# An encoder layer on one core: the fourth DRAM sum of w_o's blocks, and where the steps of the sums stand

## The chip, the cores and the metric

The kernel runs on one core of a Trainium2 chip. The metric is the device time of one execution in microseconds, the median of several runs. An engine is named as in the profile: PE (TensorE), PEld (its weight loads), DVE (VectorE), ACT (ScalarE), POOL (GpSimd), SP (SyncE, which here only issues transfers).

## The reference

One layer over 512 tokens of width 2048, all in float32:

```
h = rms_norm(x, pre_mix_g);  z = h @ w_in            # 2048 x 4096: q, k, v, u
a = chunked_attention(q, k, v, rel_bias)             # 8 heads of 128
p = multiscale_pool(u, pool_w, pool_scale)           # 4 groups of 256
m = concatenate([a, p]) @ w_o                        # 2048 x 2048
x = x + rms_norm(m, post_mix_g)
h = rms_norm(x, pre_ffn_g)
up = causal_dwconv(h @ w_up, conv_w, conv_b)         # 2048 x 11264, 3 taps
y = (gelu(up[:, :5632]) * up[:, 5632:]) @ w_down     # 5632 x 2048
x = x + rms_norm(y, post_ffn_g)
```

## The kernel before

Every float32 matrix is split into a rounded part (hi, written by ACT) and the rest (lo, written by DVE), and each product is three matmuls (`mm3`, L153 to L155). The split (L135, L136) of a weight tile needs the loaded tile (`raw4`, a ring of five) and a pair of buffers for hi and lo (`w4`, a ring of eight, so four pairs). `Weights` loads four tiles ahead: `get` of a tile first issues the load and the split of the tile four further on. A tile is 512 KB.

The stages are, in order of time: q, k, v and u projections with attention and pooling between them (the first 410 us); the product with w_o (410 to 575 us); the post-norm, the transposition back, and the first w_up products; then the w_up and w_down products, which fill the rest.

The product with w_o is made by a scheme of Strassen's kind with seven half-size products instead of eight, numbered in the order `WO = 1, 7, 2, 5, 6, 3, 4`. `wo_product(i, cc, left)` does half a product (column half `cc`, 0 or 1): four weight tiles `wo{i}_{cc}_0` to `_3`, 12 matmuls of 512 columns for each. The profile leaves numbers out, so all of them are called `wo_0` to `wo_3` there. The right factors are blocks of w_o or sums of them. Those of products 7, 5 and 6 are summed in DRAM (`wo_sum`, tiles `wt...`, in the profile `wt`). Product 4's right factor is sum 6 plus one more block. It isn't made in DRAM: `load_w` loads the block of w_o with SP, and POOL adds sum 6 to the loaded tile with an accumulating transfer (L148), before the split.

The sums in DRAM are made by a generator, `sums_in_dram`, one step at each `next(sums_step)`. A step is a copy from DRAM to DRAM, issued by SP (L251), or an accumulating transfer from DRAM onto DRAM, issued by POOL (L254), each of 1 MB. After w_o's 24 steps come 16 steps for w_down's first sums (`first_sum`, tiles `t...`, in the profile `t`), which are read near the end. The 24 steps stand among the heads of the attention, five of w_down's in the pooling stage, and the rest in the first w_up products, where `up` takes one step at each tile.

PE's instructions run in the order of the code. The other engines and queues are ordered by a scheduler, and each runs its own list in order: what stands behind a waiting instruction waits too. SP and POOL issue their transfers in such lists. `copy` is held behind the newest weight load; an add is placed where the scheduler expects its copy to be there, which may be earlier or later than its place in the code.

After product 4, for each half of the tokens (two tiles of 128): `finish` adds the product's banks to `y` (DVE, L582), squares it (ACT, L586) and scales it (DVE, L591); `norm` makes the factor, with a power on POOL (L643); `x2` updates x (DVE, L656); `turn_back` transposes x on PE (L670) and splits it into gT (L138, L139). For the first half this follows product 3, and its transposes stand between product 4's tiles in the second column half. For the second half it follows product 4, while PE does the first w_up tiles (w00) for the first half (`gate_part`). Then come the w10 tiles for all tokens.

Of the kernel before, what the change touches and what calls it, by code (L numbers as in the profile page):

```python
# [9 lines left out]
F32 = mybir.dt.float32  # L10
F32R = mybir.dt.float32r
AF = mybir.ActivationFunctionType
ALU = mybir.AluOpType
AX = mybir.AxisListType

P = 128
# [59 lines left out]
def encoder_layer(ctx: ExitStack, tc: tile.TileContext, x, xT, vecs, rel, post_mix, post_ffn,  # L76
# [7 lines left out]
    nc = tc.nc  # L84
# [8 lines left out]
    dram = ctx.enter_context(tc.tile_pool(name="dram", bufs=1, space=bass.MemoryType.DRAM))  # L93
# [7 lines left out]
    def bank(name):  # L101
        return psum.tile([P, 512], F32, tag="ps", name=name)

    def acc8(name, which, dt=F32):
        return acc.tile([P, 2048], dt, tag="acc" + which, bufs=2, name=name)

    def raw4(name):
        return big.tile([P, 1024], F32, tag="raw", bufs=5, name=name)

    def w4(name):  # L110
        return big.tile([P, 1024], F32R, tag="w4", bufs=8, name=name)
# [21 lines left out]
    def split(hi, lo, src, scale=None):  # L133
        if scale is None:
            rounded = nc.scalar.activation(hi, src, AF.Copy)  # L135
            nc.vector.tensor_sub(lo, src, f32(hi))  # L136
        else:
            rounded = nc.scalar.activation(hi, src, AF.Copy, scale=scale)  # L138
            nc.vector.scalar_tensor_tensor(lo, src, scale, f32(hi), op0=ALU.mult, op1=ALU.subtract)  # L139
        split.last = rounded.ins  # L140
        return rounded.ins

    def load_w(name, src, a, b, plus=None):
        n = a * b
        raw, hi, lo = raw4(name + "r"), w4(name + "h"), w4(name + "l")
        load_w.last = nc.sync.dma_start(raw[:, :n].rearrange("p (a b) -> p a b", a=a), src).ins
        if plus is not None:
            nc.gpsimd.dma_start(raw[:, :n].rearrange("p (a b) -> p a b", a=a), plus, accum_op=ALU.add)  # L148
        split(hi[:, :n], lo[:, :n], raw[:, :n])
        return tuple(v[:, :n].rearrange("p (a b) -> p a b", a=a) for v in (hi, lo))  # L150

    def mm3(ps, l, r, first, last):
        nc.tensor.matmul(ps, l[0], r[0], start=first, stop=False)  # L153
        nc.tensor.matmul(ps, l[0], r[1], start=False, stop=False)  # L154
        nc.tensor.matmul(ps, l[1], r[0], start=False, stop=last)  # L155
# [9 lines left out]
    def part(w, *idx):  # L165
        return tuple(v[(slice(None),) + idx] for v in w)
# [24 lines left out]
    def qk_specs(h):  # L191
        return halves(f"q{h}", w_in, head_cols("q", h), 8, P), halves(f"k{h}", w_in, head_cols("k", h), 8, P)
# [8 lines left out]


    WO = 1, 7, 2, 5, 6, 3, 4
    wo_sum = {i: [dram.tile([P, 8, 512], F32, name=f"wt{i}{cc}") for cc in range(2)] for i in (7, 5, 6)}

    def wo_block(cc, j, l):
        cs = slice(l * D // 2 + cc * 512, l * D // 2 + (cc + 1) * 512)
        return w_o[j * 1024:(j + 1) * 1024, cs].rearrange("(k p) n -> p k n", p=P)

    def wo_specs(i, cc):  # L210
        whole = wo_sum[i][cc] if i in wo_sum else wo_block(cc, *{1: (0, 0), 2: (1, 0), 3: (1, 1), 4: (1, 0)}[i])
        parts = [slice(2 * k, 2 * k + 2) for k in range(4)]
        return [(f"wo{i}_{cc}_{k}", whole[:, sl, :], 2, 512, *([wo_sum[6][cc][:, sl, :]] if i == 4 else []))
                for k, sl in enumerate(parts)]

    specs = v_specs(0)
    for h in range(1, HEADS):
        q, k = qk_specs(h)
# [24 lines left out]
    def first_block(cc, j, l):  # L243
        cs = slice(l * D // 2 + cc * S, l * D // 2 + (cc + 1) * S)
        return w_down[:2 * P * CU, cs].rearrange("(u j p) n -> p u j n", j=2, p=P)[:, :, j, :]

    def sums_in_dram():

        def copy(dest, source):
            with tc.issue_after(load_w.last):  # L250
                nc.sync.dma_start(dest, source)  # L251

        def add(dest, source):
            nc.gpsimd.dma_start(dest, source, accum_op=ALU.add)  # L254

        def wo_step(step, i, at):
            for cc in range(2):
                source = wo_block(cc, *at) if type(at) is tuple else wo_sum[at][cc]
                for k in range(2):
                    sl = slice(4 * k, 4 * k + 4)  # L260
                    step(wo_sum[i][cc][:, sl, :], source[:, sl, :])
                    yield

        for step, i, at in ((copy, 7, (1, 1)), (add, 7, (0, 1)), (copy, 5, (0, 0)), (add, 5, (0, 1)),
                            (copy, 6, 5), (add, 6, (1, 1))):
            yield from wo_step(step, i, at)
        for step, i, at in ((copy, 5, (0, 0)), (add, 5, (0, 1)), (copy, 7, (1, 1)), (copy, 6, 5),
                            (add, 7, (0, 1)), (add, 6, (1, 1)), (copy, 4, 6), (add, 4, (1, 0))):
            for cc in range(2):
                step(first_sum[i][cc], first_block(cc, *at) if type(at) is tuple else first_sum[at][cc])  # L270
                yield

    sums_step = sums_in_dram()


# [10 lines left out]
    for kb in range(KD):  # L286
        i, o = divmod(kb, 8)
        nc.sync.dma_start(xt[kb // 4][:, kb % 4, :], xT[kb * P:(kb + 1) * P, :])
        for what in "qk":
            if kb in chunks:  # L290
                raw, hi, lo = first[f"{what}0_{i}"]
                sl = slice(o * P, (o + chunks[kb]) * P)
# [4 lines left out]
        for what in "qk":  # L297
            _, hi, lo = first[f"{what}0_{i}"]
            sl = slice(o * P, (o + 1) * P)
# [7 lines left out]
    def mix(kb):  # L307
        return mixT[kb // 4][:, kb % 4, :]

    with tc.tile_pool(name="p1", bufs=2, reuse_waits="tile") as p1:  # L310
# [39 lines left out]
        def project(name, between=None):  # L350
            ps = bank(name)
            for i in range(2):
                if i and between:
                    between()
                w = weights.get(f"{name}_{i}")
                for j in range(8):
                    kb = 8 * i + j
                    mm3(ps, part(w, j), blk(hT, kb), kb == 0, kb == KD - 1)
            return ps
# [51 lines left out]
        def turn(h):  # L411
            probs = [state.pop(("p", h, t)) for t in range(NT)]
            pts = [bank(f"pt{h}_{k}") for k in range(3)]
            pts = [pts[0], pts[1][:, P:], pts[2][:, 2 * P:], pts[1][:, :P]]
            for k in (0, 1, 3, 2):
                for t in range(k, NT):
                    nc.tensor.transpose(pts[k][:, (t - k) * P:(t - k + 1) * P],
                                        probs[t][:, k * P:(k + 1) * P], ident)
            for k in range(NT):
                n, at = S - k * P, PT_AT[k] + k * P - PT_Q[k]  # L420
                split(pth[:, at:at + n], ptl[:, at:at + n], pts[k])

        def values(h):
            ps = bank(f"a{h}")
            d = slice((h % 4) * DH, (h % 4 + 1) * DH)
            for k in range(NT):
                sl = slice(PT_AT[k], PT_AT[k] + S - PT_Q[k])
                mm3(ps[:, PT_Q[k]:], part(state["v"], k, d), (pth[:, sl], ptl[:, sl]), k == 0, k == NT - 1)
            nc.scalar.activation(mix(h), ps, AF.Copy)

        def pool_proj(g, j):
            pool_keep(g, j, project(f"u{2 * g + j}"))
# [68 lines left out]
        turn(6)  # L501
        scores(7)
        pool_proj(0, 1)
        values(6)
        next(sums_step)
        pool_proj(1, 0)
        turn(7)
        pool_proj(1, 1)
        values(7)
        mixT += [acc8(f"mixT{i}", "B").rearrange("p (a b) -> p a b", a=4) for i in (2, 3)]  # L510
        pool_mix(0, keep_mix)
# [22 lines left out]

        def wo_product(i, cc, left, between=None):
            ps = [bank(f"m{i}{cc}{t}") for t in range(2)]
            for q in range(4):
                w = weights.get(f"wo{i}_{cc}_{q}")
                for j in range(2):
                    kb = 2 * q + j  # L540
                    for t in range(2):
                        mm3(ps[t], tuple(v[:, kb, t * P:(t + 1) * P] for v in left), part(w, j), kb == 0, kb == 7)
                if between:
                    between(q)
            return ps
# [13 lines left out]
    with tc.tile_pool(name="p2", bufs=1, reuse_waits="tile") as p2:  # L559
# [116 lines left out]
        whole = slice(0, D // 2)  # L676
# [165 lines left out]
    with tc.tile_pool(name="p3", bufs=2, reuse_waits="tile") as p3:  # L842
# [13 lines left out]
        def gate(u, z):  # L856
            a = p3.tile([P, 2, S], F32, tag="ca", name="ca")
            for j in range(2):
                taps(z[:, j, :], 2 * u + j, a[:, j, :])
            nc.scalar.activation(flat(a), flat(a), AF.Gelu_apprx_tanh)  # L860
            return a
# [13 lines left out]
        def normed(ps):  # L875
            z = new_z()
            for j in range(2):
                nc.vector.tensor_mul(z[:, j, :], ps[j], R)
            return z
# [207 lines left out]
        a = gate(1, normed(z))  # L1087
# [3 lines left out]
        a = gate(2, normed(z))  # L1091
# [272 lines left out]
```

## Time and profile before

| | |
|---|---|
| runs | 1932.14 us median of 3 (1931.54 to 1932.59) |
| profiled execution | 1932.79 us, its span from first to last instruction 1931.0 us |
| granted TensorE clock | 0.996 |
| PE busy | 1899.8 us of the span |
| DVE, ACT, POOL busy | 1432.8, 915.5, 285.3 us |
| DMA | 386.90 MB, mean 200 GB/s |

Busy time is what the engine's instructions took. A row of a timeline has the start and the duration in us, the engine, the line of the code, the operation, what is written and read, how many instructions the row holds, and in brackets how long the engine was idle before it and what ended that. A row of the windows has the window, its length, the busy time and the number of instructions of PE, PEld, DVE, ACT and POOL, the granted clock, the DMA share (the mean busy share of the core's 16 DMA engines) and GB/s. DMA rows name what is written and read, and the time from issue to landing.

### The profile page before, as it was taken

What the parts mean: (1) busy time and instruction counts of PE and PEld (TensorE: products, weight loads), DVE (VectorE), ACT (ScalarE), POOL (GpSimd) and SP (SyncE); (2) the same over time, 40 slices, a digit from 0 to 9 for tenths busy, and PEclk for the clock granted to TensorE, in tenths of its full rate; (3) what the DMA queues carried; (4) which work ended last, traced back from release to release, by engine and by line L of the source; (5) the groups of instructions that cost most, each with busy time, mean ns of one, the idle gap of its engine ahead of it and who ended that gap; (6) DMA issues with size and microseconds to landing.
All of it is one profiled execution on the core that took longest, in us unless ns stands there. A gap on an engine that the chain in (4) does not pass through costs nothing.

```text
span 1931.0 us, 28650 instructions
## 1 busy us (share of the span) xinstructions
PE 1899.8 (98%) x11566; PEld 1707.9 (88%) x11566; DVE 1432.8 (74%) x1618; ACT 915.5 (47%) x1126; POOL 285.3 (15%) x369
## 2 busy tenths in 40 slices
PE   9999999999979999999999999999999899999998
PEld 7888888888868889999999999999999688888886
DVE  5455345587668756887878878788788799998877
ACT  6333233356445434544544445444454655455543
POOL 5110010000010101111111111111110112222221
PEclk9999999999999999999999999999999999999999
DMA  7598395447695957667676676766766999999997
GB/s 244 162 259 217 120 264 142 133 148 250 188 305 184 287 144 162 155 170 188 150 188 157 168 188 150 186 161 166 188 162 196 324 265 250 255 210 240 227 222 238
DMA packets 182789, 386.90 MB, mean 200 GB/s; under 512 B 10944, under 2 KB 62528, under 8 KB 178624
## 3 DMA queue, kind: packets, MB, share of 16 engines
q1 hardware_dynamic: 132704, 249.79, 38.0%
q0 software_dynamic: 49952, 135.28, 37.1%
q8 instruction: 90, 1.47, 0.3%
q14 instruction: 43, 0.35, 0.1%
HBM read 328.40 MB, written 98.57 MB: 221 GB/s over the span
## 4 chain that ended last, share of the span: by engine, by line
PE 92%; DMA 3%; issue 2%; DVE 1%; ACT 1%; SPq 0%; POOL 0%; POOLq 0%; DVEq 0%; ACTq 0%
PE q L154 14%; PE q L153 14%; PE q L155 14%; PE p L155 6%; PE p L153 6%; PE p L154 6%; PE up L154 2%; PE up L155 2%; PE up L153 2%; PE m L153 2%; PE m L154 2%; PE m L155 2%; PE u L153 2%; PE v L153 2%; PE u L154 2%
## 5 line engine op out<-in xcount | busy, mean ns | idle before, releaser
L154 PE MATMUL q<-gTl,wfh 128*128 128x256 f32 x1216 | 344.1, 283 | 0.0
L155 PE MATMUL q<-gTh,wfl 128*128 128x256 f32 x1216 | 344.1, 283 | 0.0
L153 PE MATMUL q<-gTh,wfh 128*128 128x256 f32 x1216 | 344.1, 283 | 0.0
L153 PEld LDWEIGHTS q<-gTh,wfh 128*128 128x128 f32 x1216 | 233.5, 192 | 0.0
L154 PEld LDWEIGHTS q<-gTl,wfh 128*128 128x128 f32 x1216 | 233.5, 192 | 0.0
L155 PEld LDWEIGHTS q<-gTh,wfl 128*128 128x128 f32 x1216 | 233.5, 192 | 0.0
L153 PE MATMUL p<-bh,ah 128*128 128x512 f32 x560 | 219.3, 392 | 4.5 <-ACT ah L135 4.5
L154 PE MATMUL p<-bl,ah 128*128 128x512 f32 x560 | 219.1, 391 | 2.3 <-DVE bl L136 2.3
L155 PE MATMUL p<-bh,al 128*128 128x512 f32 x560 | 219.5, 392 | 1.7 <-DVE al L136 1.7
L135 ACT ACTIVATE wfh<-wx 128x1024 fp32r<-128x1024 f32 x152 | 159.9, 1056 | 119.1 <-PE q L154 91.4
L136 DVE TENSOR_TENSOR wfl<-wx,wfh 128x1024 fp32r<-128x1024 f32 x152 | 183.9, 1220 | 33.5 <-ACT wfh L135 33.4
L135 ACT ACTIVATE wfh<-wy 128x1024 fp32r<-128x1024 f32 x76 | 80.6, 1061 | 119.3 <-PE q L154 105.8
L135 ACT ACTIVATE bh<-b 128x2048 fp32r<-128x2048 f32 x56 | 106.9, 1917 | 61.3 <-DVE b L785 40.6
L136 DVE TENSOR_TENSOR bl<-b,bh 128x2048 fp32r<-128x2048 f32 x56 | 127.7, 2287 | 10.5 <-PE p L154 8.5
L153 PEld LDWEIGHTS p<-bh,ah 128*128 128x128 f32 x560 | 105.8, 189 | 27.1 <-ACT ah L135 5.3
L155 PEld LDWEIGHTS p<-bh,al 128*128 128x128 f32 x560 | 105.9, 189 | 24.8 <-DVE al L136 2.9
L997 POOL DMA_DIRECT2D wx<-in_w_up x76 | 67.5, 888 | 408.3 <-DVE wfl L136 381.5
L154 PEld LDWEIGHTS p<-bl,ah 128*128 128x128 f32 x560 | 105.8, 189 | 24.8 <-DVE bl L136 2.6
L136 DVE TENSOR_TENSOR wfl<-wy,wfh 128x1024 fp32r<-128x1024 f32 x76 | 92.9, 1223 | 32.2 <-ACT wfh L135 30.9
L837 POOL DMA_DIRECT2D sum<-part x60 | 72.7, 1231 | 251.4 <-DVE part L828 109.3
L136 DVE TENSOR_TENSOR wfl<-wz,wfh 128x1024 fp32r<-128x1024 f32 x38 | 46.6, 1225 | 59.7 <-ACT wfh L135 59.7
L153 PE MATMUL q<-h4h,wfh 128*128 128x256 f32 x304 | 86.0, 283 | 0.0
(590 smaller groups left out, 4953.7 us busy)
## 6 DMA issues: line engine op xcount, KB each, us to landing
wx<-in_w_up POOLq DMA_DIRECT2D x76, 512.0 KB, 7.0
sum<-part POOLq DMA_DIRECT2D x70, 512.0 KB, 8.2
b<-in_w_down SPq DMA_DIRECT2D x32, 1024.0 KB, 8.9
wx<-in_w_up SPq DMA_DIRECT2D x40, 512.0 KB, 6.1
wy<-in_w_up SPq DMA_DIRECT2D x38, 512.0 KB, 5.5
wz<-in_w_up SPq DMA_DIRECT2D x38, 512.0 KB, 7.0
wy<-in_w_up POOLq DMA_DIRECT2D x38, 512.0 KB, 7.4
wt<-in_w_o POOLq DMA_DIRECT2D x12, 1024.0 KB, 12.2
```

Of the source, the lines that this page charges most:

```text
L135: rounded = nc.scalar.activation(hi, src, AF.Copy)
L136: nc.vector.tensor_sub(lo, src, f32(hi))
L153: nc.tensor.matmul(ps, l[0], r[0], start=first, stop=False)
L154: nc.tensor.matmul(ps, l[0], r[1], start=False, stop=False)
L155: nc.tensor.matmul(ps, l[1], r[0], start=False, stop=last)
L837: nc.gpsimd.dma_start(dest, v, accum_op=ALU.add)
L997: nc.gpsimd.dma_start(self.raw[k, what], self.block(k, m, kh), accum_op=ALU.add)
```

## The change

Product 4's right factor becomes a fourth sum in DRAM: a copy of sum 6 and an add of the block, in four pieces of each, so eight steps more in front of w_down's. `load_w` loses its accumulating transfer, and product 4's tiles are loaded from `wt` like those of 7, 5 and 6. Three calls of `next(sums_step)` are added in the pooling stage and one in each second half (`cc` = 1) of w_o's products, ten in all.

```diff
-    def load_w(name, src, a, b, plus=None):
+    def load_w(name, src, a, b):
...
-        if plus is not None:
-            nc.gpsimd.dma_start(raw[:, :n].rearrange("p (a b) -> p a b", a=a), plus, accum_op=ALU.add)
         split(hi[:, :n], lo[:, :n], raw[:, :n])
...
-    wo_sum = {i: [dram.tile([P, 8, 512], F32, name=f"wt{i}{cc}") for cc in range(2)] for i in (7, 5, 6)}
+    wo_sum = {i: [dram.tile([P, 8, 512], F32, name=f"wt{i}{cc}") for cc in range(2)] for i in (7, 5, 6, 4)}
...
-        return [(f"wo{i}_{cc}_{k}", whole[:, sl, :], 2, 512, *([wo_sum[6][cc][:, sl, :]] if i == 4 else []))
+        return [(f"wo{i}_{cc}_{k}", whole[:, sl, :], 2, 512)
...
         for step, i, at in ((copy, 7, (1, 1)), (add, 7, (0, 1)), (copy, 5, (0, 0)), (add, 5, (0, 1)),
-                            (copy, 6, 5), (add, 6, (1, 1))):
+                            (copy, 6, 5), (add, 6, (1, 1)), (copy, 4, 6), (add, 4, (1, 0))):
...
         pool_proj(0, 1)
+        next(sums_step)
         values(6)
         next(sums_step)
         pool_proj(1, 0)
+        next(sums_step)
         turn(7)
         pool_proj(1, 1)
+        next(sums_step)
...
             ps = [bank(f"m{i}{cc}{t}") for t in range(2)]
+            if cc:
+                next(sums_step)
```

The lists of PE, DVE and ACT hold the same instructions in the same order as before. Those of SP and POOL change.

POOL from the pooling stage's last memsets to the first w_up products, before (`us` are the pooling's sums, `small` the norm's factors, `rt` those of the next norm, `t_106` and `t_107` are w_down's sum 7 for the second column half and sum 6 for the first):

```order
L444 MEMSET us 128x4
L148 DMA wo_0_0r<-wt_101 128x1024
L148 DMA wo_0_1r<-wt_101 128x1024
...
L148 DMA wo_1_2r<-wt_102 128x1024
L643 TENSOR_TENSOR small<-small,mhalf 128x2
L148 DMA wo_1_3r<-wt_102 128x1024
L643 TENSOR_TENSOR small<-small,mhalf 128x2
L176 TENSOR_TENSOR rt<-rt,mhalf 128x4
L254 DMA t_106<-in_w_down 512x1x512
L254 DMA t_107<-in_w_down 512x1x512
```

The same after (here `t_105` to `t_108` are sums 5 and 7, each for both column halves, `t_109` and `t_110` sum 6):

```order
L442 MEMSET us 128x4
L252 DMA t_105<-in_w_down 512x1x512
L252 DMA t_106<-in_w_down 512x1x512
L252 DMA t_107<-in_w_down 512x1x512
L252 DMA t_108<-in_w_down 512x1x512
L646 TENSOR_TENSOR small<-small,mhalf 128x2
L252 DMA t_109<-in_w_down 512x1x512
L646 TENSOR_TENSOR small<-small,mhalf 128x2
L174 TENSOR_TENSOR rt<-rt,mhalf 128x4
L252 DMA t_110<-in_w_down 512x1x512
```

The eight transfers onto product 4's tiles are gone, and five adds of w_down's sums stand in their place, four ahead of the first norm's power and one between the two.

SP from the last tile of product 3 to the second half's x, before (`w00` are the first w_up tiles, `x2` a tile of x):

```order
L146 DMA wo3_1_3r_4282<-in_w_o 128x2x512
L146 DMA wo4_0_0r_4309<-in_w_o 128x2x512
...
L146 DMA wo4_1_3r_4467<-in_w_o 128x2x512
L146 DMA w00_0r_4499<-in_w_up 128x2x512
L146 DMA w00_1r_4535<-in_w_up 128x2x512
L650 DMA x2_4653<-in_x 128x2048
```

The same after:

```order
L146 DMA wo3_1_3r_4292<-in_w_o 128x2x512
L249 DMA t71_108<-in_w_down 512x1x512
L146 DMA wo4_0_0r_4320<-wt40_103 128x1024
...
L146 DMA wo4_1_3r_4471<-wt41_104 128x1024
L249 DMA t60_109<-t50_105 16x16384
L146 DMA w00_0r_4503<-in_w_up 128x2x512
L146 DMA w00_1r_4539<-in_w_up 128x2x512
L653 DMA x2_4657<-in_x 128x2048
```

Product 4's tiles come from the new sums `wt40` and `wt41`, and a copy of w_down's sums stands ahead of them and one behind.

POOL in the pooling stage, around the softmax of the last head (`s`, one memset for each of its four tiles) and the first memset of the pooling (`u`), before:

```order
L254 DMA t_103<-in_w_down 512x1x512
L399 MEMSET s 64x64 x4
L254 DMA t_104<-in_w_down 512x1x512
L437 MEMSET u 128x16
L399 MEMSET s 64x64 x4
```

The same after:

```order
L252 DMA wt_103<-in_w_o 128x4x512
L397 MEMSET s 64x64 x4
L252 DMA wt_103<-in_w_o 128x4x512
L252 DMA wt_104<-in_w_o 128x4x512 x2
L397 MEMSET s 64x64
L435 MEMSET u 128x16
L397 MEMSET s 64x64 x3
```

Four adds into the new sum stand where two adds of w_down's stood, three of them directly ahead of the last head's memsets.

More of the change, by code (lines that the diff above doesn't have):

```diff
@@ L210, in wo_specs @@
     def wo_specs(i, cc):
-        whole = wo_sum[i][cc] if i in wo_sum else wo_block(cc, *{1: (0, 0), 2: (1, 0), 3: (1, 1), 4: (1, 0)}[i])
+        whole = wo_sum[i][cc] if i in wo_sum else wo_block(cc, *{1: (0, 0), 2: (1, 0), 3: (1, 1)}[i])
         parts = [slice(2 * k, 2 * k + 2) for k in range(4)]
-        return [(f"wo{i}_{cc}_{k}", whole[:, sl, :], 2, 512, *([wo_sum[6][cc][:, sl, :]] if i == 4 else []))
+        return [(f"wo{i}_{cc}_{k}", whole[:, sl, :], 2, 512)
                 for k, sl in enumerate(parts)]
```

## The prediction

> **What bounds the kernel now.** I read the page's first part, then the table of windows over the stage around w_o's products, then TensorE's rows there with their idle time, then the chain that ended last.
>
> ```profile
> PE 1899.8 (98%) x11566; PEld 1707.9 (88%) x11566; DVE 1432.8 (74%) x1618; ACT 915.5 (47%) x1126; POOL 285.3 (15%) x369
> ...
> 490.00:510.00 20.00, 20.00 (x90) 16.57 (x89) 9.90 (x9) 9.16 (x10) 0.00 (x0) 1.00 0.58 190
> ...
> 530.00:550.00 20.00, 18.18 (x78) 14.01 (x76) 10.13 (x10) 5.79 (x10) 3.68 (x5) 1.00 0.99 240
> 550.00:570.00 20.00, 14.86 (x70) 11.17 (x71) 13.96 (x16) 7.64 (x13) 2.63 (x3) 1.00 1.04 314
> 570.00:590.00 20.00, 17.24 (x119) 15.88 (x118) 17.29 (x31) 15.28 (x34) 0.71 (x1) 0.91 0.66 252
> 590.00:610.00 20.00, 17.41 (x133) 15.92 (x133) 15.61 (x29) 13.59 (x28) 1.01 (x1) 1.00 0.45 160
> 610.00:630.00 20.00, 20.00 (x89) 16.54 (x89) 19.85 (x19) 6.91 (x7) 2.37 (x2) 1.00 0.86 251
> ```
>
> TensorE is busy for 1899.8 of 1931.0 us. So a shorter time can come only from its 31 idle us. The windows (length, then busy time of PE, PEld, DVE, ACT and POOL, the granted clock, the DMA share) show where 12.3 of them lie: from 530 to 610 us PE lacks 1.82, 5.14, 2.76 and 2.59. Before and behind, it is full. Here stand product 4 of w_o, the norm behind it and the first w_up products. In the first half DVE and ACT are idle too, and the DMA engines are full (0.99, 1.04): everything waits for data.
>
> ```profile
> 546.54 0.50 PE L154 MATMUL m<-wo_2l,a22h 128*128 128x512 f32 x1 [0.77 <-DVE wo_2l L136]
> ...
> 550.34 0.51 PE L153 MATMUL m<-wo_3h,a22h 128*128 128x512 f32 x1 [1.02 <-ACT wo_3h L135]
> ...
> 569.14 1.49 PE L670 MATMUL xt<-ident,x 128*128 128x128 f32 x8 [3.49 <-DVE y L582]
> ...
> 578.57 0.35 PE L153 MATMUL up<-gTh,w_0h 128*128 128x256 f32 x1 [2.45 <-DVE gTl L139]
> ...
> 593.83 0.38 PE L153 MATMUL up<-gTh,w_0h 128*128 128x256 f32 x1 [1.74 <-ACT gTh L138]
> ```
>
> PE waits for product 4's split tiles, then for DVE (L582, L139), which is late because the same tiles hold it up: its queue is in order, and the tiles' splits stand ahead of the norm's work. The chain names the root, three accumulating transfers out of the DRAM sums:
>
> ```profile
> 526.01 8.00 DMA wo_0r<-wt
> ...
> 545.60 10.04 DMA wo_1r<-wt
> ...
> 557.04 9.02 DMA wo_3r<-wt
> ```
>
> **Part 1: product 4's second transfer goes.** Each of its eight tiles is loaded by SP and then added to by POOL, one behind the other, 8 to 10 us for the second alone. How long a tile may take is seen in product 3, where nothing is added:
>
> ```profile
> 498.02 0.38 SPq L146 DMA_DIRECT2D wo_0r<-in_w_o  x1
> ...
> 509.24 1.06 ACT L135 ACTIVATE wo_0h<-wo_0r 128x1024 fp32r<-128x1024 f32 x1 [1.66 <-PE m L154]
> ...
> 517.43 0.39 PE L153 MATMUL m<-wo_0h,s4h 128*128 128x512 f32 x1
> ...
> 539.19 0.39 PE L153 MATMUL m<-wo_0h,a22h 128*128 128x512 f32 x1
> ```
>
> The load is issued at 498.02, its split waits only for PE (a free buffer) until 509.24, and PE uses it at 517.43: 19.4 us, of which the two splits need about 2.4 (1.06 on ACT, then much the same on DVE). So a load may land up to 17 us after its issue and PE never notices. A load and an accumulation in series, in full DMA engines, pass that; a load alone does not. I take product 4 to run like product 3 afterwards, 21.76 us for its eight tiles (539.19 less 517.43).
>
> What PE must do from there to the first product over all tokens (the first w10 tile) follows from rows of before:
>
> ```profile
> 581.54 0.28 PE L153 MATMUL up<-gTh,w_1h 128*128 128x256 f32 x1
> ...
> 584.42 0.28 PE L153 MATMUL up<-gTh,w_2h 128*128 128x256 f32 x1
> ...
> 590.18 1.91 PE L670 MATMUL xt<-ident,x 128*128 128x128 f32 x16
> ...
> 609.59 0.40 PE L153 MATMUL up<-gTh,w_0h 128*128 128x512 f32 x1
> ```
>
> Product 4 takes 21.8 us, eight half-width gate parts 2.88 each (584.42 less 581.54), together 23.0, and 64 transposes 4 x 1.9 = 7.6. That is 52.4 us, against the 70.4 us that the stretch takes now (539.19 to 609.59). The difference, 18.0 us, is the ceiling of the gain. It holds the half-speed clock behind the 3.49 us wait (granted clock 0.91 over 20 us, 1.8 us).
>
> Not all of it comes, since the norm of the second token half is a chain of its own:
>
> ```profile
> 574.35 0.40 PE L155 MATMUL m<-wo_3h,a22l 128*128 128x512 f32 x1
> ...
> 579.51 1.28 DVE L582 TENSOR_TENSOR y<-m,y 128x512 f32<-128x512 f32 x2
> ...
> 587.45 5.39 DVE L656 SCALAR_TENSOR_TENSOR x<-y,small,x 128x512 f32<-128x512 f32 x8
> ...
> 592.26 1.06 ACT L586 ACTIVATE junk<-x 128x1024 f32<-128x1024 f32 x1 [1.51 <-DVE x L656]
> ```
>
> Behind product 4's last matmul come DVE's add (579.51), the norm, x's update (587.45), a square on ACT that the next gTh stands behind (592.26), and the gate parts. From that add to 609.59 it takes 30.1 us. I keep these 30.1 us, since each link is work. What changes is when the add can start. Product 4 can end at 539.2 + 21.8 + three groups of eight transposes at 0.95 = 563.9. Now DVE comes to the add 4.8 us behind the last matmul. Afterwards it has less queued: by the order, the split of w_up's third tile (1.2) and four gTl (0.4 each), some 2.8 us, part of which falls before 563.9. If the add starts at once, w10 starts at 594.0 and 15.6 us are gained; with the old 4.8 us of delay (579.51 less 574.7), 10.8. I take 2.0 us of delay: w10 starts at 596.0, a gain of **13.6 us**. From 610 us on PE is full, so the rest moves up as a whole.
>
> The other link is the first half's norm, which product 4's transposes need. Its add on DVE came at 546.4, behind the split of wo_2; it can then come at 539.4 when product 3 ends, x's update starts some 8 us later (as from 579.51 to 587.45), and half of 5.39 us on, at 550, the half that the first transposes read is there. They are due behind five tiles, at 539.2 + 13.6 = 552.8. That is covered by 2.8 us.
>
> **Part 2: four copies and four adds more, in the stage of the pooling projections.** They take the places of five steps of w_down's sums, and three places more. PE is full there, and I cost them at nothing: the cover is the prefetch by four tiles of 24 matmuls, some 22 us (0.227 each, 21.76 over 96). SP's copies wait for the adds into sum 6, which land long before; a copy's own place in SP's queue takes 0.58 us, at worst 4.1, ahead of a load:
>
> ```profile
> L251 SPq DMA_DIRECT2D t<-in_w_down x4: 567/584/4126, 273.7 to 612.8; - x4
> ```
>  POOL's queue has three adds right ahead of the last head's memsets, and each waits for its copy:
>
> ```profile
> 319.48 0.14 POOL L399 MEMSET s<- 64x64 f32 x1 [2.28 <-DVE s L397]
> ```
>
> If the last copy, issued near 311, lands 13 us later, this memset and DVE behind it are held by 5 us, a quarter of what the split weights cover.
>
> **Part 3: seven steps of w_down's sums among w_o's products.** By the order, four copies and four adds of 1 MB run before product 4 starts, one of each beside it (an add that is written later goes as soon as its copy is there). On PE, DVE and ACT nothing stands in another place. SP's loads stand behind the copies (0.58 us each, as above); on POOL only the two powers of the norms wait, each behind an add. Their price is DMA time:
>
> ```profile
> q1 hardware_dynamic: 1840, 1.84, 60.8%
> ...
> t<-in_w_down SPq DMA_DIRECT2D x1, 1024.0 KB, 6.1
> ...
> q0 software_dynamic: 528, 1.05, 41.5%
> ...
> 408.00:430.00 22.00, 22.00 (x99) 18.22 (x98) 19.58 (x23) 11.78 (x14) 0.10 (x1) 1.00 0.62 194
> 430.00:470.00 40.00, 40.00 (x178) 33.15 (x177) 31.03 (x29) 26.68 (x32) 0.00 (x0) 1.00 0.77 269
> 470.00:495.00 25.00, 25.00 (x112) 20.68 (x112) 14.99 (x13) 12.61 (x15) 0.00 (x0) 1.00 0.62 202
> 495.00:518.00 23.00, 23.00 (x103) 19.07 (x102) 12.37 (x13) 10.06 (x11) 0.00 (x0) 1.00 0.59 191
> 518.00:540.00 22.00, 22.00 (x99) 18.23 (x98) 18.45 (x14) 9.45 (x15) 2.70 (x3) 1.00 0.77 193
> ```
>
> The first line is a 9 us window with one copy and 0.79 MB of loads: 5.5 us of all engines. A wo tile of 0.52 MB costs 1.6 us (0.59 x 23 for eight and a half), so the loads take 2.4 and the copy 3.1. The third is a 16 us window with one add: 6.6 us. The windows from 408 to 540 use 13.6 + 30.8 + 15.5 + 13.6 + 16.9 = 90 of 132 us, and some 7 of the last are accumulations that go. 83 + 4 x 9.7 = 122 us fit into 132. But 430 to 470 comes to 40.5 of 40 and 495 to 540 to 43 of 45, so loads there land later. The worst landing of a 512 KB load beside full engines that I found is
>
> ```profile
> 240.00:270.00 30.00, 30.00 (x142) 25.19 (x141) 13.89 (x25) 9.79 (x17) 5.53 (x8) 1.00 1.07 273
> ...
> k_1r<-in_w_in SPq DMA_DIRECT2D x1, 512.0 KB, 13.1
> ```
>
> and 13.1 is under the 17 us above. So I cost Part 3 at nothing as well; its ends are 0 and the backlog that the third rival gives. The Trainium skill's page "DMA: Bandwidth & Descriptors" (section "Measured (HBM→SBUF, 128 partitions, SWDGE, issued from GpSimd)") has 6.15 us for 1 MB. By it the eight transfers would be an estimated 49 us and the stage exactly full, 132 of 132; no row here shows a plain copy that dear, so the trace's prices stand.
>
> In w_up's first products five copies and five adds become three and three, where PE does not wait: nothing.
>
> **The sum.** 13.6 us off. The profiled execution took 1932.79 us (span 1931.0), 0.65 above the median of 1932.14; both move alike, so the forecast against the median is 1932.1 - 13.6 = **1918.5 us**.
>
> **Rivals.**
>
> *The chain on DVE is as late as before.* The delay of 4.8 us stays, or x's first half is not ready at 553 and the transposes wait. For it: DVE is busy for 17.29 of 20 us in that window. Against: it was busy for only 10.13 and 13.96 of 20 in the windows before, while the work piled up behind late tiles. The gain is 8 to 10.8 us: 1921 to 1924.
>
> *The DMA engines become the bound in w_o's products*, the case on the slower side. If copies and adds cost twice the price (19.4 a pair), 495 to 540 would need 62 of 45 us. Loads would then fall 17 us behind, the whole 17 us of slack is used, and from there each further us of DMA work stalls PE; the norm's power, behind the add of sum 6, comes late too. It decides from about 20 a pair on: the stage then needs 83 + 80 = 163 of 132 us, and 31 - 17 = 14 us of stall meet the 13.6 gained. At 22 a pair it is 171, and 22 of stall: 1940. For it: transfers in full engines took 10 us and more. Against: that is time to landing while sharing; the engines' own time is 3.1 and 6.6.
>
> *POOL's waits in the pooling stage* reach PE: the memset of the last head is held until the turn of that head. It would take over 20 us of delay; I give it a loss of 0 to 6 us, 1918 to 1924.
>
> *The wait is only partly the accumulation's:* loads alone are late too because the x loads and stores fill the engines. Then only what PE lacks from 530 to 570 comes back, 1.82 + 5.14 = 7 us: 1925. Against: the accumulations (the software queue) take 0.583 of the engines from 525 to 560.
>
> ```profile
> q0 software_dynamic: 1007, 3.67, 58.3%
> ```
>
> **How the numbers follow.** Forecast, 1914 to 1921: 0.62. The late chain: 0.18. DMA-bound with only part of the gain lost: 0.06, with all of it: 0.05. POOL: 0.04. Partly the accumulation's: 0.05. The low end of the range is the ceiling (1932.1 - 18.0 = 1914), the high end 1924, with the second rival's whole span; 0.84 lies inside by these chances. About 0.2%, 4 us, is what a measurement can tell. Faster by more: 0.92; within: 0.04; slower: 0.04.
>
> **What would show it.** Right: PE rows of product 4 without waits, product 4 ending near 564, w10 starting near 596, no half clock behind 570, PE still full from 408 to 539, tiles of product 4 landing within 13 us. Wrong: splits (L135) that wait for a DMA in products 2, 3 or 4, a POOL power that waits behind an add, or DVE's add well behind the product's last matmul.

## The result, and the profile after

| | before | after |
|---|---|---|
| runs | 1931.84 us median of 4 (1931.42 to 1932.59) | 1915.67 us median of 4 (1914.48 to 1916.42) |
| ratio | | 0.9914, 95% interval 0.9899 to 0.9930 |
| profiled execution, its span | 1932.79, 1931.0 us | 1915.74, 1913.9 us |
| first product of the first w10 tile | 609.59 us | 594.19 us |

The change makes the kernel 16.2 us faster; 13.6 were forecast. One of the ten runs of the doubled steps, further down, was slow (3131.39 us at a granted clock of 0.556), and the ratio there leaves it out. First the page's rows of busy time and DMA traffic of the kernel after. PE is busy for 1894.7 us where it was 1899.8. So of the 17.1 us by which the span fell, 12.0 are idle time that is gone (31.2 to 19.2), and 5.1 are busy time. Some 4.6 of these 5.1 lie between 540 us and w10 (57.3 us busy before, 52.7 after): the half clock of before (0.91 from 570 to 590 us, 1.8 us), and matmuls that took longer beside the waits (0.50 us in the prediction's row at 546.54, where others take 0.39).

```profile
PE 1894.7 (99%) x11566; PEld 1706.7 (89%) x11566; DVE 1431.8 (75%) x1618; ACT 915.6 (48%) x1126; POOL 282.6 (15%) x365
...
DMA packets 183301, 391.09 MB, mean 204 GB/s; under 512 B 10944, under 2 KB 62528, under 8 KB 178624
```

The windows of the kernel after, with the columns of the prediction's (length, busy time of PE, PEld, DVE, ACT and POOL, granted clock, DMA share, GB/s):

```profile
408.00:540.00 132.00, 132.00 (x584) 109.41 (x583) 99.81 (x92) 73.26 (x87) 4.75 (x5) 1.00 0.88 276
...
430.00:470.00 40.00, 40.00 (x178) 33.17 (x177) 31.04 (x29) 26.48 (x32) 1.17 (x1) 1.00 0.97 323
...
495.00:518.00 23.00, 23.00 (x103) 19.05 (x102) 12.37 (x13) 10.24 (x11) 1.16 (x1) 1.00 0.92 275
518.00:540.00 22.00, 22.00 (x99) 18.23 (x98) 21.85 (x18) 12.16 (x18) 1.16 (x1) 1.00 0.89 268
...
530.00:550.00 20.00, 20.00 (x90) 16.58 (x89) 19.02 (x21) 10.56 (x18) 2.77 (x2) 1.00 1.00 328
550.00:570.00 20.00, 20.00 (x129) 17.88 (x128) 18.16 (x28) 17.67 (x37) 0.00 (x0) 1.00 1.03 337
570.00:590.00 20.00, 18.50 (x146) 17.26 (x146) 14.73 (x32) 11.72 (x24) 1.71 (x2) 1.00 0.57 223
590.00:610.00 20.00, 19.97 (x104) 17.06 (x104) 19.89 (x21) 8.11 (x9) 1.21 (x1) 1.00 0.55 167
```

From 530 to 570 us PE lacked 6.96 us before and lacks nothing now, although the DMA engines are as full there (1.00, 1.03) as they were (0.99, 1.04). The clock of 0.91 behind 570 us is 1.00. What PE still lacks, 1.5 us from 570 to 590, are mostly two waits for ACT's gTh (0.67 and 0.40 us). From 408 to 540 us the DMA engines are used for 116 of 132 us (0.88), for 38.8 of 40 in the second row and for 40.7 of 45 in the two behind it, and PE is full all the way.

TensorE's rows of the kernel after at product 4's first matmul, its last one, the first gate part and the first w10 tile; then DVE's add of the first and of the second token half:

```profile
539.00 0.39 PE L151 MATMUL m<-wo_0h,a22h 128*128 128x512 f32 x1
...
563.22 0.39 PE L153 MATMUL m<-wo_3h,a22l 128*128 128x512 f32 x1
...
564.24 0.36 PE L151 MATMUL up<-gTh,w_0h 128*128 128x256 f32 x1
...
594.19 0.40 PE L151 MATMUL up<-gTh,w_0h 128*128 128x512 f32 x1
```

```profile
538.52 1.37 DVE L585 TENSOR_TENSOR y<-m,y 128x512 f32<-128x512 f32 x2
...
564.12 1.28 DVE L585 TENSOR_TENSOR y<-m,y 128x512 f32<-128x512 f32 x2
```

None of product 4's matmuls waits, and no split on ACT waits for a transfer between 430 and 600 us; before, all eight of product 4's did, for 0.9 to 4.7 us. The product ends at 563.6, and DVE's add starts 0.5 us behind that, where it came 4.8 us behind it before. From the add to w10 it takes 30.07 us (594.19 less 564.12), as it did.

DMA issues of the kernel after from 525 to 545 us (count, KB each, median us to landing); `t` is one of w_down's sums, to which POOL adds:

```profile
wo_1r<-wt SPq DMA_DIRECT2D x2, 512.0 KB, 4.9
t<-in_w_down POOLq DMA_DIRECT2D x1, 1024.0 KB, 12.5
...
wo_3r<-wt SPq DMA_DIRECT2D x2, 512.0 KB, 7.1
wo_0r<-wt SPq DMA_DIRECT2D x1, 512.0 KB, 7.8
```

Product 4's eight tiles land in 5 to 9 us (4.8 to 8.9), with an add of 1 MB beside them.

### The profile page after: what moved, and what is told of

Its sections match the earlier page's. It is cut to its first block, busy times and chain, and to the rows that moved or that the text cites. A ratio compares the mean times of both kernels' runs of the same rounds, so it can differ in the third digit from the quotient of the medians.

```text
span 1913.9 us, 28637 instructions
## 1 busy us (share of the span) xinstructions
PE 1894.7 (99%) x11566; PEld 1706.7 (89%) x11566; DVE 1431.8 (75%) x1618; ACT 915.6 (48%) x1126; POOL 282.6 (15%) x365
## 4 chain that ended last, share of the span: by engine, by line
PE 95%; issue 2%; DVE 1%; DMA 1%; ACT 1%; SPq 0%; POOL 0%; POOLq 0%; DVEq 0%; ACTq 0%
PE q L152 15%; PE q L153 15%; PE q L151 15%; PE p L153 6%; PE p L152 6%; PE p L151 6%; PE m L152 3%; PE m L151 3%; PE m L153 3%; PE up L152 2%; PE up L153 2%; PE up L151 2%; PE u L152 2%; PE v L152 2%; PE u L153 2%
## 5 line engine op out<-in xcount | busy, mean ns | idle before, releaser
L136 DVE TENSOR_TENSOR wfl<-wy,wfh 128x1024 fp32r<-128x1024 f32 x76 | 93.0, 1224 | 32.5 <-ACT wfh L135 31.2
L152 PE MATMUL q<-h7l,wfh 128*128 128x256 f32 x304 | 86.1, 283 | 0.0
```

## The experiments

Theory: the gain is that a tile no longer needs two transfers in series, the second of them accumulating; the steps moved among w_o's products and into the pooling stage are free. The rivals are the prediction's: the DVE chain, DMA-bound loads, POOL, and a wait that is only partly the accumulation's. All ratios are against the kernel before, beside which each was run.

**The changed kernel without the steps among w_o's products.**

```diff
             ps = [bank(f"m{i}{cc}{t}") for t in range(2)]
-            if cc:
-                next(sums_step)
```

> The changed kernel without its seven steps among w_o's products: w_down's 16 first-sum steps all stand in the first w_up products. Theory (the gain comes from product 4's tile no longer being added to after its load): 1915 to 1918 us, product 4 without waits on PE, the first w10 matmul near 594 us; the three copy-add pairs more in w_up's first products (some 29 us of DMA time) cost nothing, since PE has a tile of 5.4 us there and a tile's load needs 1.6. Rival (the gain, or part of it, comes from moving w_down's steps out of the full DMA engines at 610 to 670 us): 1920 to 1930 us, with PE waiting for loads behind 600 us.

Measured: 1916.95 us (1915.50 to 1917.72), ratio 0.9917 (0.9902 to 0.9932). The window over w_o's products, which has a DMA share of 0.88 in the kernel after:

```profile
408.00:540.00 132.00, 132.00 (x584) 109.31 (x583) 99.91 (x92) 73.27 (x87) 0.10 (x1) 1.00 0.65 213
```

PE is full in both. The seven places are worth nothing measurable, either way. The two DMA shares give the price of the moved work: 0.23 x 132 = 30.4 us for four copies and four adds, 7.6 a pair.

**The kernel before with those places alone.** It tells whether the steps would gain or cost anything without the new sum.

```diff
             ps = [bank(f"m{i}{cc}{t}") for t in range(2)]
+            if cc:
+                next(sums_step)
```

> The kernel before with only the seven step places among w_o's products added (product 4 still loads its tile and adds to it). Theory: not faster, 1931 to 1937 us: three copies and three adds more meet the stage from 408 to 540 us, 90 + 29 of 132 us of DMA time, and the accumulations on product 4's tiles are at best as late as before. Rival (the step places bring the gain): 1918 to 1925 us.

Measured: 1932.41 us (1930.46 to 1934.26, 10 runs), ratio 0.9999 (0.9989 to 1.0008). Three of TensorE's waits, in product 4, for DVE's add and for gTl:

```profile
546.18 0.50 PE L154 MATMUL m<-wo_2l,a22h 128*128 128x512 f32 x1 [0.76 <-DVE wo_2l L136]
...
568.42 1.25 PE L672 MATMUL xt<-ident,x 128*128 128x128 f32 x8 [3.08 <-DVE y L584]
...
577.85 0.36 PE L153 MATMUL up<-gTh,w_0h 128*128 128x256 f32 x1 [2.44 <-DVE gTl L139]
```

The waits for product 4's splits and for DVE are those of the kernel before. So the whole gain belongs to the new sum.

**The kernel before without product 4's second transfer.** The load stays, nothing takes the transfer's place, so sum 6 is missing from product 4's right factor.

```diff
-        return [(f"wo{i}_{cc}_{k}", whole[:, sl, :], 2, 512, *([wo_sum[6][cc][:, sl, :]] if i == 4 else []))
+        return [(f"wo{i}_{cc}_{k}", whole[:, sl, :], 2, 512, *([]))
```

> The kernel before with product 4's accumulating transfers left out and nothing in their place (sum 6 is missing in product 4's right factor). Theory: as fast as the changed kernel, 1915 to 1918 us; this is what Part 1 alone is worth, with Parts 2 and 3 at nothing. Rival (the new places of the steps carry part of the gain): 1920 us or more. If this is faster than the changed kernel by over 1 us, the sum in DRAM or the moved steps cost something.

Measured: 1917.95 us (1916.91 to 1918.53), ratio 0.9923 (0.9908 to 0.9937). TensorE's row at w10, and the window over product 4:

```profile
594.36 0.40 PE L153 MATMUL up<-gTh,w_0h 128*128 128x512 f32 x1
```

```profile
540.00:570.00 30.00, 30.00 (x172) 26.12 (x171) 27.18 (x38) 22.60 (x45) 1.58 (x1) 1.00 0.89 315
```

w10 starts within 0.2 us of the kernel after (594.19), and PE is full. So the second transfers are the whole cause, and the four copies and four adds that replace them cost nothing that these runs can tell.

**The kernel before, with a plain second transfer.** The same two transfers in series for each tile, the same bytes loaded, but the second does not accumulate, so product 4's right factor is sum 6 alone.

```diff
-            nc.gpsimd.dma_start(raw[:, :n].rearrange("p (a b) -> p a b", a=a), plus, accum_op=ALU.add)
+            nc.gpsimd.dma_start(raw[:, :n].rearrange("p (a b) -> p a b", a=a), plus)
```

> The kernel before with product 4's second transfer as a plain copy onto the tile, issued by POOL behind the load, not an accumulation (product 4's right factor is then sum 6 alone). It keeps the series of two transfers and takes away what the accumulation itself costs. Theory (two transfers in series pass the 17 us of slack only because the accumulations, 2.9 us of all engines each, fill the engines and land 8 to 10 us late): a plain copy costs about 1.6, lands in 5 to 6, so 10 to 12 us in series fit, and most of the gain is there: 1916 to 1921 us. Rival (the series itself, with POOL's wait for each load in an in-order queue, is what holds PE): 1926 to 1932 us.

Measured: 1921.72 us (1920.73 to 1925.46), ratio 0.9947 (0.9930 to 0.9963), between the two. The landing of two of the second transfers (520 to 545 us), TensorE's waits behind product 4 and w10, and DVE's add of the first token half and then of the second:

```profile
wo_0r<-wt POOLq DMA_DIRECT2D x2, 512.0 KB, 6.4
```

```profile
565.17 0.63 PE L670 MATMUL xt<-ident,x 128*128 128x128 f32 x4 [1.14 <-DVE gTl L139]
568.24 0.36 PE L153 MATMUL up<-gTh,w_0h 128*128 128x256 f32 x1 [2.44 <-DVE gTl L139]
599.24 0.40 PE L153 MATMUL up<-gTh,w_0h 128*128 128x512 f32 x1
```

```profile
541.56 1.28 DVE L582 TENSOR_TENSOR y<-m,y 128x512 f32<-128x512 f32 x2
...
569.18 1.28 DVE L582 TENSOR_TENSOR y<-m,y 128x512 f32<-128x512 f32 x2
```

The eight plain transfers land in 5.2 to 7.6 us where the accumulating ones took 6.6 to 10.6. That is enough for product 4 itself: no matmul of it waits. But its splits still come late enough to hold DVE's queue. The first half's add starts 3.0 us later than in the kernel after, the second half's 5.1 us later, and PE waits 2.44 us for gTl. Of the 15.2 us by which w10 moves when the second transfer goes, 10.3 are there once it does not accumulate (609.59 to 599.24), and 4.9 are the price of two transfers in series. What makes the 10.3 was not taken apart: it may be the accumulation's own longer landing, or the engine time that it takes from the loads (from 525 to 560 us POOL's queue took 0.58 of the DMA engines before and 0.34 here). Here the rival of the late DVE chain can be seen at work: with PE's waits in the product gone, DVE alone holds the rest.

**The changed kernel with twice the steps among w_o's products.** Fourteen places instead of seven, to find where the DMA engines become the bound.

```diff
-            if cc:
-                next(sums_step)
+            next(sums_step)
```

> The changed kernel with a step in both halves of each w_o product, 14 in place of seven. By the order, four copies and four adds of 1 MB then run between 430 and 495 us, where the windows of before use 46 of 65 us of DMA time. Theory (a copy costs 3.1 and an add 6.6 us of all engines, and a load may land 17 us late): 46 + 39 = 85 of 65, 20 us of backlog, so some 3 us of PE waits in products 2, 5 or 6: 1917 to 1922 us. Rival A (the DMA-bound rival of the prediction, transfers at about twice that price): 46 + 78 = 124 of 65, 42 us of stall, over 1950 us. Rival B (such transfers slow no load, since the loads' queue has its own share of the engines): 1915 to 1917 us with no PE waits.

Measured: 1929.25 us (median of 10; nine of them 1925.53 to 1931.06), ratio 0.9983 (0.9974 to 0.9993): some 13 us of the gain are lost. It is the rival of the full DMA engines, at a load that the price of 9.7 us a pair had put 3 us over the line. Its DMA engines are full from 450 to 495 us, where the kernel after has a share of 0.59 from 470 on:

```profile
450.00:470.00 20.00, 20.00 (x90) 16.57 (x89) 11.60 (x11) 9.12 (x10) 2.31 (x2) 1.00 1.06 335
470.00:495.00 25.00, 23.89 (x105) 19.19 (x104) 12.28 (x11) 11.64 (x14) 2.31 (x2) 1.00 1.01 313
```

The weight loads that are issued from 453 to 496 us land in 11 to 19 us, where those of the kernel after take 4 to 6. Below are SP's issues of a tile `wo_0` and of a `wo_1` five tiles on, ACT's splits of both, DVE's split of the first, and PE's first use of both:

```profile
464.28 0.32 SPq L146 DMA_DIRECT2D wo_0r<-wt  x1
...
485.47 0.32 SPq L146 DMA_DIRECT2D wo_1r<-wt  x1
```

```profile
483.12 1.06 ACT L135 ACTIVATE wo_0h<-wo_0r 128x1024 fp32r<-128x1024 f32 x1 [2.19 <-DMA wo_0r<-wt]
...
500.27 1.06 ACT L135 ACTIVATE wo_1h<-wo_1r 128x1024 fp32r<-128x1024 f32 x1 [5.51 <-DMA wo_1r<-wt]
```

```profile
484.21 1.23 DVE L136 TENSOR_TENSOR wo_0l<-wo_0r,wo_0h 128x1024 fp32r<-128x1024 f32 x1 [0.96 <-ACT wo_0h L135]
```

```profile
484.23 0.50 PE L151 MATMUL m<-wo_0h,n1h 128*128 128x512 f32 x1 [0.35 <-ACT wo_0h L135]
...
501.38 0.69 PE L151 MATMUL m<-wo_1h,s2h 128*128 128x512 f32 x1 [2.17 <-ACT wo_1h L135]
```

The first tile lands 18.8 us after its issue (464.28 to 483.12), and PE waits 1.1 us for its two splits (0.35, and 0.76 for DVE's). So a load may land about 17.7 us after its issue: the prediction's 17 holds for one tile. It does not hold for a row of them. A late split frees its buffer late. DVE's split of that tile ends at 485.44 (484.21 and 1.23) and SP issues the `wo_1` at 485.47, five tiles on, the length of the ring of loaded tiles; in the kernel after, that load is issued at 480.47. It lands in 14.8 us and is still late, and PE waits 2.7 us more. The window of this kernel over these waits:

```profile
495.00:518.00 23.00, 20.25 (x76) 15.79 (x75) 11.55 (x11) 9.45 (x10) 0.00 (x0) 0.85 0.94 291
```

The clock of 0.85 over 23 us costs 3.4 us more, nearly as much as the waits of 3.9. Product 4's last matmul stands at 570.21, 7.0 us behind that of the kernel after. A second stall follows, in which the first w_up loads land late and DVE's split of `w_2` holds the gTl behind it in the queue:

```profile
572.02 1.06 ACT L135 ACTIVATE w_2h<-w_2r 128x1024 fp32r<-128x1024 f32 x1 [2.23 <-DMA w_2r<-in_w_up]
...
573.11 1.23 DVE L136 TENSOR_TENSOR w_2l<-w_2r,w_2h 128x1024 fp32r<-128x1024 f32 x1 [3.02 <-ACT w_2h L135]
...
574.88 0.36 PE L151 MATMUL up<-gTh,w_0h 128*128 128x256 f32 x1 [3.39 <-DVE gTl L139]
...
605.89 0.40 PE L151 MATMUL up<-gTh,w_0h 128*128 128x512 f32 x1
```

w10 comes 11.7 us later than in the kernel after. The sum of DMA time did not foretell this. With the 7.6 us a pair measured above in place of 9.7, the expectation's sum is 46 + 30 = 76 of 65 us; the backlog of 11 us lies under the slack of 17, and PE would not wait. Over the whole of 408 to 540 us the engines are busy for 120 of 132 us (0.91), hardly more than the 116 of the kernel after. What differs is that here a whole row of loads lands late; the ring, the clock and the in-order queues then pass it on.

**The changed kernel without the three places added in the pooling stage.**

```diff
         pool_proj(0, 1)
-        next(sums_step)
         values(6)
         next(sums_step)
         pool_proj(1, 0)
-        next(sums_step)
         turn(7)
         pool_proj(1, 1)
-        next(sums_step)
```

> The changed kernel without the three added places in the pooling stage: the last adds of sum 4 fall into w_o's first products, and w_down's first sums stand mostly in w_up. Theory (the places cost and bring nothing, the cover is the prefetch by four tiles): 1915 to 1917.5 us, PE full from 300 to 560. Rival (the three adds that hold POOL ahead of the last head's memsets cost PE something that is hidden in the 1915.7): 1913 to 1915. Rival (sum 4 is late for product 4): over 1920, with splits of product 4 waiting for its loads.

Measured: 1916.74 us (1914.48 to 1917.58), ratio 0.9918 (0.9901 to 0.9934). POOL in the kernel after (first row) waits 16.21 us for the last copy and holds the last head's memsets; in this kernel (second row) they wait for DVE alone:

```profile
325.14 1.26 POOL L252 DMA_DIRECT2D wt<-in_w_o  x1 [16.21 <-DMA wt<-wt]
```

```profile
318.92 0.14 POOL L397 MEMSET s<- 64x64 f32 x1 [2.27 <-DVE s L395]
```

The hold of some 6 us is real, and PE does not see it: the time is the same.

**The changed kernel with the second half's squares later.** In the kernel after, ACT's squares of the updated x stand ahead of the last gTh, and PE waits for those. Here they are held behind the gate's splits.

```diff
+                turned = split.last
...
-        keep_x(2)
+        with tc.issue_after(turned):
+            keep_x(2)
```

> The changed kernel with the squares of x's second half (ACT, L589) held behind the last of its transposed splits, so that they no longer stand ahead of gTh. Theory (the 2.8 us that the stretch from product 4 to w10 still lacks are ACT's squares ahead of gTh): the first gate part of the second half goes from 5.1 to about 3 us and starts half a us earlier, w10 starts near 592: 1.5 to 2.5 us faster than the changed kernel's 1915.7, so 1913 to 1914.5. Rival (the squares are then late for the next norm, or the moved splits and differences on DVE delay w_up's first tiles): 1915.5 or more.

Measured: 1914.76 us (1912.91 to 1915.22), ratio 0.9909 (0.9894 to 0.9924). In its trace DVE's add and w10 stand here:

```profile
564.78 1.28 DVE L585 TENSOR_TENSOR y<-m,y 128x512 f32<-128x512 f32 x2
```

```profile
592.21 0.40 PE L151 MATMUL up<-gTh,w_0h 128*128 128x512 f32 x1
```

The chain from the add to w10 is 27.43 us instead of 30.07. That is 2.6 us, too little for four runs to tell, so both kernels were run again, one after the other on one chip.

> The changed kernel as it is, on the same chip and among the same runs as the kernel with the later squares. Theory: its median lies at 0.991 to 0.992 of the kernel before, and its first half-clock window in w_down's first products may or may not fall as in the first profile (one stretch of 6.8 us). If the 1.5 us by which its span moved more than the first w10 tile come from where those windows fall by chance, this profile may show two separate windows and a span near 1915.5 us; if they belong to the change, it shows one stretch again and a span near 1914 us.

> The changed kernel with the update-square chain of the second token half freed: the squares of x's two last tiles are issued behind the gate's splits, as in the run before it. Theory: w10 starts some 2 us earlier than in the changed kernel (near 592.2 us in the trace), from there on PE is full, so the median is 1.5 to 2.5 us under the changed kernel's of the same call (0.9990 of it). Rival: the later squares collide with the first full w10 tiles or their power on POOL comes late further on, and what was gained is given back: same median within 0.5 us.

Measured: the kernel after 1917.18 us (1916.22 to 1917.97, 5 runs), ratio 0.9924 (0.9911 to 0.9938); with the squares later 1913.79 us (1912.08 to 1917.20, 4 runs), ratio 0.9908 (0.9894 to 0.9921). The chain is again 30.07 us in the one (563.41 to 593.48) and 27.44 in the other (567.00 to 594.44). Over both sets of runs the means are 1916.5 us of nine runs and 1914.3 of eight, 2.1 us apart, with an interval of about 0.6 to 3.7. Taken from the one chip alone, five and four runs, the means differ by 3.0 us, and the scatter is too wide to tell that from nothing. So the version with the later squares is probably the fastest, by little: the pooled runs say so, and the chain is 2.6 us shorter in both of its profiles. Both speak against the rival that the gain is given back.

Its w10 at 594.44 is no earlier than the other's, against the expectation, since the profiled execution was the slowest of its four (1917.20 us) and had lost about 3 us before. The first 20 us of this execution, and then of the kernel after in its first profile:

```profile
0.00:20.00 20.00, 16.57 (x59) 12.81 (x60) 13.29 (x25) 13.63 (x23) 1.90 (x38) 0.91 0.89 285
```

```profile
0.00:20.00 20.00, 17.96 (x72) 14.29 (x73) 14.68 (x27) 14.88 (x24) 1.90 (x38) 1.00 0.91 300
```

A start with longer waits and a stretch at half clock. It is scatter between executions and not the edit, since the same edit had 18.42 us of PE and a clock of 1.00 there in its first profile.

## Why the prediction was right, and where its terms were off

*The bound.* Right in the main. PE's idle time around product 4 was the second transfers', but for the 1.5 us of waits that stay: taken away alone, they move w10 to 594.36, the kernel after's place. The rival of a wait that is only partly the accumulation's, 1925 us, falls. Loads alone land in time beside engines that are just as full. Two readings were off. That a shorter time can come only from PE's 31 idle us was too narrow, since 5.1 of the 17.1 us were busy time; the prediction's own ceiling of 18.0 us is more than the 12.3 idle us of its windows. And the second transfers took 6.6 to 10.6 us to land, not 8 to 10.

*Part 1.* The mechanism is as the prediction put it: product 4 without waits, its end at 563.6 (563.9 forecast), the first half's x in time, no half clock behind 570. The kept chain of 30.1 us was 30.07 in the kernel after, 30.06 with the plain transfers and 30.07 in the second profile, so it does not hang on what stands ahead of it. But not each link of it is needed: with ACT's squares moved it is 27.43. The term that was mis-sized is the delay of DVE's add: 2.0 us assumed, 0.5 measured. DVE had caught up before product 4 ended, since the splits of w_up's first tiles fell beside the product (the third at 561.41). The assumption kept some of the old backlog where its cause was gone: of the 2.8 us that the prediction saw queued, all but 0.5 us ran before the product ended. That puts w10 at 594.2 instead of 596.0, a gain of 15.4 instead of 13.6.

*The rest of the difference.* The span fell by 17.1 us, 1.7 more than w10. From 610 us (before) and 594 us (after) PE is full for 875 us in both. The difference arises in the first w_down products, where the DMA engines are full in both kernels and PE waits. There the clock falls to half in windows that lie differently. Two rows of 8 us each, of the kernel before, of the kernel after, and of the same code in its second profile:

```profile
1499.00:1507.00 8.00, 5.37 (x16) 4.09 (x17) 6.42 (x4) 4.69 (x4) 1.26 (x2) 0.79 1.01 379
...
1515.00:1523.00 8.00, 5.08 (x14) 3.75 (x15) 7.14 (x7) 4.66 (x3) 0.00 (x0) 0.79 0.71 235
```

```profile
1484.00:1492.00 8.00, 6.06 (x15) 4.51 (x16) 6.02 (x4) 4.29 (x3) 1.16 (x2) 0.57 1.01 385
...
1500.00:1508.00 8.00, 5.29 (x22) 4.09 (x23) 7.20 (x6) 4.67 (x3) 0.00 (x0) 1.00 0.68 224
```

```profile
1484.00:1492.00 8.00, 6.61 (x15) 4.96 (x16) 5.31 (x4) 3.58 (x2) 0.45 (x1) 0.57 1.01 403
...
1500.00:1508.00 8.00, 6.24 (x20) 4.72 (x21) 7.25 (x7) 5.44 (x4) 0.00 (x0) 0.79 0.66 203
```

Two executions of the same code differ: one has no half clock at 1500, the other has. From the first w_down product to the next stage they take 392.6 and 393.8 us, the kernel before 394.0. So a microsecond or so of the 16.2 is where these windows fell and can't be put to the change; in the second set of runs the kernel after gained 14.9 us (1932.10 less 1917.18). What sets their place wasn't tried. The Trainium skill's page "TensorE: Matmul & The Clock Gate" (section "Part 1: The HAM clock gate") has the clock judged in free-running windows of 3413 ns that do not start with the kernel, so that the place varies from run to run. The rows agree: 0.79 over 8 us is 3.4 us at half clock (8 x 0.21 x 2), 0.57 is 6.9, two windows.

*Part 2.* Cost nothing, as forecast. The hold of POOL's memsets was forecast at 5 us; POOL's wait of 16.21 us ended at 325, and the memset that ran at 319.48 before ran at 325.88, 6.4 us. Taken away, the time is the same.

*Part 3.* Cost nothing, as forecast. The price of a pair was too high: 7.6 us instead of 9.7, so the stage used 116 of 132 us, not 122. The adds are near the forecast, and the copies make up most of the difference. Over 405 to 540 us the software queue, which holds the four adds alone, took 18.4% of the engines, 6.2 us each (6.6 forecast):

```profile
q0 software_dynamic: 2112, 4.19, 18.4%
```

That leaves 1.4 us for a copy (3.1 forecast, from one window of 9 us; why that window gave more stays open). The margin to the rival of the full DMA engines was misjudged the other way. The prediction let it decide where the stage needs 163 of 132 us, with 17 us of slack for every load. The doubled steps lost 13 us with the engines busy for 120 of the same 132. The slack belongs to one late tile; a row of late tiles eats it through the ring. So that Part 3 cost nothing was in part luck: its reason, a sum with a slack, would have let the doubled steps pass with 3 us of loss or none.

*The rivals.* The DVE chain as late as before didn't come, but the plain second transfer shows its mechanism, at 4.9 us. POOL's waits stay off the path.

## What to carry to other kernels

Where a tile is loaded and then added to by a second transfer, look at what stands behind its split in the in-order queues: here the product's own waits and the norm's lateness had the same cause, and making the sum ahead in DRAM took both away. When a wait goes, work out the delay of the next engine from its queue without that cause rather than keeping part of the old one. Free DMA time in a stage holds moved transfers only while no run of loads lands later than its slack: buffer rings pass a late landing on to the next issue, so spread the steps, and look at how long the loads take to land and not at the sum of DMA time alone (in w_o's products landings of up to 10.5 us cost nothing here, and a row of 11 to 19 us cost 13).

## What was not expected of the hardware

- An accumulating transfer of 512 KB onto a loaded tile landed in 6.6 to 10.6 us beside full DMA engines (0.99 and 1.04); the same transfer without accumulation in 5.2 to 7.6.
- A copy of 1 MB from DRAM to DRAM took about 1.4 us of all DMA engines, worked out from the shares above, less than a load of 512 KB (1.6 us); an accumulating transfer of 1 MB in DRAM took 6.2.
- In the doubled steps, waits of 2.2 and 0.6 us for one tile came with some 6.8 us at half clock (0.85 over 23 us), and 3.9 us of waits cost 7.0 us. A longer wait in the same execution, 3.39 us at 574.88, was followed by none (1.00 from 560 to 580).
